# Four gate groups as a seven-product block in a hybrid decoder layer

## The chip, the cores and the metric

The kernel runs on one core of a Trainium2 chip. The metric is the device time in microseconds of one execution. TensorE (PE in the profile) multiplies matrices and accumulates into PSUM; VectorE (DVE), ScalarE (ACT) and GpSimd (POOL) work element by element; SyncE (SP) issues most of the transfers, in order, on one queue.

## The reference

One decoder layer over 1024 positions of 1024 features, in float32. Cut to what matters here:

```python
h = rms_norm(x, norm_mix_g)
y_m = mlstm_branch(h)             # 4 heads, chunks of 128 positions, state carried from chunk to chunk
y_d = diff_attention(h)           # 8 heads, causal
y_c = memory_cross_attention(h, mem)
g_m, g_d, g_c = split(sigmoid(h @ w_gate + b_gate), 3)    # w_gate is 1024 x 3072
merged = g_m*(y_m @ w_proj_m) + g_d*(y_d @ w_proj_d) + g_c*(y_c @ w_proj_c)
x = x + merged @ w_out
x = x + square(relu(rms_norm(x) @ w_up)) @ w_down
```

The gates are `h @ w_gate`, 3072 columns in 12 groups of 256 columns. Groups 0 to 3 belong to the mLSTM branch, 4 to 7 to the attention, 8 to 11 to the memory branch.

## The kernel before

Every float32 product is made of three matmuls: each operand is split into a high part (a cast on ACT to the type that TensorE multiplies fast) and a low part (a subtraction on DVE), and `mm3` adds high x high, high x low and low x high. `hT` holds the transposed h in both parts for all 8 k tiles (64 KB of each partition).

**Gate groups.** `gate_steps` is a generator: a gate group is 2 tiles of 128 columns x 2 halves of 512 positions = 4 accumulations of 8 k tiles x 3 matmuls (96 matmuls of 128x128 by 128x512), one step for each k tile. ACT takes the tanh of each accumulation and SP stores it in `gates` in HBM. The groups serve as filler for TensorE between steps of the branches that wait for other engines. `gate_steps((2, 1, 1, 2, 6))` gives the runs: groups 0 and 1 in the memory branch, 2 inside the mLSTM branch, 3 as its last part (positions 544 to 576), 4 and 5 between mLSTM branch and attention, 6 to 8 inside the attention, and 9 to 11 behind it. `gate_load` loads a group's weights and splits them (128x256 a tile).

**The mLSTM branch.** `branch_m` weaves a stream of TensorE steps with items at written-out positions (`weave`). The last of eight parts (head 0, second half) has its projections at positions 480 to 544, and its `krows`, `scores` and four `chunk`s at 528, 536 and 547 to 559. A chunk needs the split state `Ch` of the chunk ahead (tiles `C`, `Ch`) and the split weights `mpT`. The weights of all projections pass through one pool `wpm` of 25 tiles.

**The attention.** `branch_d` runs 8 heads with the projections of the next heads, then gate steps, as filler. Its pools (k and q tiles `dk`, `dq`; values `dv`; the mask; weights `daT`) lie in the memory above `hT` and the weight pools.

**The tail.** `tail` projects the three branch outputs, memory branch first. `k_tiles` loads eight y tiles of 512 KB through two buffers (`kraw`) and splits each (`kt`, ACT cast and DVE subtraction of 128x1024). The first weight group runs with its k loop outside, so that each k tile feeds 12 matmuls as it comes. Its tiles lie in the memory of `hT` and of the attention's pools. The MLP behind it already uses a form in which a 2x2 block product is made of seven products instead of eight (`PROD`, `wino`).

**Order.** Where `pinned` is set, TensorE runs in program order. Within the rest a planner orders each engine's queue, SP's and POOL's included, by program order and by its own estimate of when an instruction can start. A tile that reuses memory waits until the tiles there before it have been used for the last time; with `reuse_waits="tile"` a pool waits tile by tile.

Of the kernel before, what the change touches and what calls it, by code (L numbers as in the profile page):

```python
# [10 lines left out]
F32 = mybir.dt.float32  # L11
F32R = mybir.dt.float32r
# [19 lines left out]
def f32(ap):  # L32
    return ap.bitcast(F32)
# [38 lines left out]
class Layer:  # L72
# [359 lines left out]
    def gate_load(self, pool=None):  # L432

        pool = pool or self.gwp
        n = self.gate_n
        if n == 12 * NK:
# [131 lines left out]
    def branch_m(self, pool, gp, tail, gnext):  # L568
# [397 lines left out]
    def branch_d(self, pool):  # L966
# [143 lines left out]
                combine(s)  # L1110
        fill(8)
        norm(15, 2)
        assert self.gdone <= 288
        while self.gdone < 288:
            next(gates)
        self.pinned = False


# [497 lines left out]
    def run(self):  # L1616
        tc, nc = self.tc, self.nc
        with ExitStack() as ctx:
# [19 lines left out]
            self.x1d = dt("x1_d", (8, P, D))  # L1638
            self.h2d = dt("h2_d", (8, P, D))
            self.rd = dt("r_d", (16, P, 7, 512))  # L1640
            with ExitStack() as c1:
                E1 = lambda *x, **k: c1.enter_context(tc.tile_pool(*x, **k))
                self.pmm = E1(name="pmm", bufs=1, space=PSUM)
                self.ptp = E1(name="ptp", bufs=2, space=PSUM)
                self.psc = E1(name="psc", bufs=2, space=PSUM)
                hp = E1(name="hp", bufs=1)
                self.hT = hp.tile([P, NK, 2, S], F32R, name="hT")
                with ExitStack() as c2:
                    E2 = lambda *x, **k: c2.enter_context(tc.tile_pool(*x, **k))
                    kv = E2(name="kv", bufs=1)  # L1650
                    self.wp = E2(name="wp", bufs=4)
                    self.rp = E2(name="rp", bufs=3)
                    with tc.tile_pool(name="ptmp", bufs=1) as tmp0, tc.tile_pool(name="ptmp2", bufs=2) as tmp, tc.tile_pool(name="ptmp8", bufs=8) as tmp8:
                        class T:
                            def tile(_, shape, dt, tag, name):
                                p = tmp8 if tag == "xk" else tmp if tag in ("mx", "sq", "r1", "r4") else tmp0
                                return p.tile(shape, dt, tag=tag, name=name)
                        self.phase_x(kv, T())
                    self.gates = self.gate_steps((2, 1, 1, 2, 6))
                    with tc.tile_pool(name="pc", bufs=2) as pc, tc.tile_pool(name="pc1", bufs=1) as pc1, tc.tile_pool(name="pc3", bufs=5) as pc3, tc.tile_pool(name="pc4", bufs=6) as pc4, tc.tile_pool(name="wpc", bufs=8) as self.gwp, tc.tile_pool(name="rpc", bufs=2) as self.grp:  # L1660
                        class T2:
                            def tile(_, shape, dt, tag, name):
                                p = {"cpe": pc4, "cpT": pc3, "cscr": pc1, "gt": pc1, "cqT": pc1}.get(tag, pc)
                                return p.tile(shape, dt, tag=tag, name=name)
                        self.gpool = T2()
                        self.branch_c(T2())
                cg = ExitStack()
                gnext = cg.enter_context(tc.tile_pool(name="wgn", bufs=8, side="right"))
                with ExitStack() as c2:
                    E2 = lambda name, bufs: c2.enter_context(tc.tile_pool(name=name, bufs=bufs, reuse_waits="tile"))  # L1670
                    gm, pm3, self.rp, self.wp = E2("gm", 1), E2("pm3", 3), E2("rpm", 3), E2("wpm", 25)
                    pm1, pm = E2("pm1", 1), E2("pm", 2)
                    class T3:
                        def tile(_, shape, dt, tag, name):
                            p = pm3 if tag == "pre" else pm if tag in ("tho", "cv", "Ch", "C", "hss", "den") else pm1
                            return p.tile(shape, dt, tag=tag, name=name)
                    self.gpool, self.gwp, self.grp = T3(), self.wp, self.rp
                    self.branch_m(T3(), gm, 1, gnext)
                with tc.tile_pool(name="wpg", bufs=13, reuse_waits="tile") as self.wp, tc.tile_pool(name="rpg", bufs=3, reuse_waits="tile") as self.rp:
                    self.gwp, self.grp = self.wp, self.rp  # L1680
                    with tc.tile_pool(name="pg", bufs=2) as self.gpool:
                        for _ in range(2 * 32):
                            next(self.gates)
                    cg.close()
                    with tc.tile_pool(name="pd", bufs=2) as pd, tc.tile_pool(name="pd3", bufs=3) as pd3, tc.tile_pool(name="pdm", bufs=1) as pdm, tc.tile_pool(name="pd5", bufs=7) as pd5, tc.tile_pool(name="pdv", bufs=5) as pdv, tc.tile_pool(name="pdv2", bufs=17) as pdv2, tc.tile_pool(name="pd4", bufs=4) as pd4:
                        self.tmask = pdm.tile([P, D], F32, name="tmask")
                        nc.gpsimd.memset(self.tmask, 0.0)
                        nc.gpsimd.affine_select(
                            out=self.tmask[:, D - P : D], in_=self.tmask[:, D - P : D], pattern=[[-1, P]],
                            compare_op=ALU.is_ge, fill=NEG, base=0, channel_multiplier=1,  # L1690
                        )
                        class T4:
                            def tile(_, shape, dt, tag, name):
                                tag = "dscr2" if tag == "gt" else tag
                                p = pd5 if tag == "draw" else pdv if tag == "drr" else pdv2 if tag == "dv" else pd4 if tag in ("dk", "dkl") else pdm if tag == "dpe1" else pd3 if tag in ("daT", "dst") else pdm if tag in ("dscr", "dscr2", "y", "dsg") else pd
# [12 lines left out]
def pack(i):  # L1708
# [25 lines left out]
        return q.transpose(3, 2, 1, 0, 4)  # L1734

    wg = i["w_gate"][0]
    w["wgate"] = np.stack([grp(wg, r(256 * g, 256)) for g in range(12)])
# [33 lines left out]
```

## Time and profile before

| | |
|---|---|
| runs | 2205.79, 2208.11, 2208.55 us, median 2208.11 |
| profiled execution | 2207.4 us, of which the span from the first to the last instruction is 2205.3 |
| granted TensorE clock | 0.995 |
| busy in the span | PE 2162.5, PEld 1862.0, DVE 1360.7, ACT 982.2, POOL 525.2 us |
| HBM | read 178.76 MB, written 67.14 MB |

PEld is TensorE's weight load, which overlaps its matmuls. A row of the timeline has the start and the length in us, the engine, the line of the kernel, the operation, the tile written `<-` the tiles read with their shapes, a count where equal rows are merged, and in brackets how long the engine had been idle and what ended it. A row of a window has each engine's busy time in that stretch. A group's row ends with its count, then the busy time and the mean in ns, then the idle time ahead of it. In the view of a tile three durations are minimum, median and maximum in ns. A row of a transfer has its count, the size of one and the median us from issue to landing.

### The profile page before, as it was taken

How to read it: one execution, taken by the hardware profiler on the slowest of the kernel's cores; microseconds unless marked ns; L12 is line 12 of the kernel's file. 1: busy time of each engine (PE TensorE's matmuls, PEld its weight loads, DVE VectorE, ACT ScalarE, POOL GpSimd, SP SyncE). 2: the span in 40 equal slices, each digit the busy share in tenths (PEclk: the TensorE clock that was granted, in tenths of full speed). 3: DMA queues.
4: the chain of work that ended last, by engine and by line, in shares of the span. 5: the costliest groups of instructions: out<-in, count | busy, mean ns of one | idle time of the engine just before them, and what ended most of it. 6: DMA issues, size and time to landing. Idle time of an engine off the chain costs nothing.

```text
span 2205.3 us, 30616 instructions
## 1 busy us (share of the span) xinstructions
PE 2162.5 (98%) x11097; PEld 1862.0 (84%) x11097; DVE 1360.7 (62%) x2598; ACT 982.2 (45%) x1962; POOL 525.2 (24%) x696
## 2 busy tenths in 40 slices
PE   7999999999999999999999999999999999999999
PEld 5878888898899999999888888887787888788887
DVE  6643565565237777777641242544588877767779
ACT  6543354454336666666542120314444444543332
POOL 2100000000011111111000002102657655555553
PEclk9999999999999999999999999999999999999999
DMA  7123122121333333333343443436435444854444
GB/s 250 31 78 117 52 92 73 43 81 44 108 109 91 89 87 88 89 90 82 101 153 114 133 161 107 144 103 207 157 106 197 158 150 146 321 195 154 145 140 167
DMA packets 127948, 273.06 MB, mean 124 GB/s; under 512 B 12945, under 2 KB 21430, under 8 KB 125750
## 3 DMA queue, kind: packets, MB, share of 16 engines
q1 hardware_dynamic: 125494, 258.53, 37.2%
q10 hardware_dynamic: 2304, 12.58, 1.4%
q8 instruction: 87, 1.43, 0.3%
q14 instruction: 63, 0.52, 0.1%
HBM read 178.76 MB, written 67.14 MB: 112 GB/s over the span
## 4 chain that ended last, share of the span: by engine, by line
PE 86%; DVE 5%; DMA 4%; ACT 2%; issue 2%; POOL 1%; SPq 0%; DVEq 0%; ACTq 0%; POOLq 0%
PE mm L91 51%; PE p L91 22%; PE sc L91 6%; PE po L91 3%; PE tp L94 3%; DVE acc L67 1%; PE pr L94 1%; DVE wo L67 1%; DVE u L67 0%; DVE w L112 0%; DMA kraw<-y 0%; PE tp L91 0%; DMA wraw<-in_wdown 0%; DVE xts L67 0%; DMA xr<-h_d 0%
## 5 line engine op out<-in xcount | busy, mean ns | idle before, releaser
L91 PE MATMUL mm<-w,hT 128*128 128x384 f32 (+3 forms) x2496 | 471.7, 331 | 2.5 <-ACT w L111 2.4
L91 PE MATMUL mm<-hT,w 128*128 128x512 f32 x1920 | 465.6, 395 | 0.0
L91 PEld LDWEIGHTS mm<-hT,w 128*128 128x128 f32 x1920 | 353.6, 188 | 74.0
L91 PEld LDWEIGHTS mm<-w,hT 128*128 128x128 f32 x2496 | 389.0, 189 | 13.8 <-ACT w L111 3.2
L91 PE MATMUL p<-xo,wo 128*128 128x512 f32 x1344 | 311.0, 393 | 6.4 <-DVE st L1418 3.2
L91 PE MATMUL p<-xd,wo 128*128 128x512 f32 x1344 | 309.5, 392 | 5.5 <-DVE c L67 2.2
L91 PEld LDWEIGHTS p<-xo,wo 128*128 128x128 f32 x1344 | 253.0, 189 | 63.1 <-DVE u L67 3.7
L91 PEld LDWEIGHTS p<-xd,wo 128*128 128x128 f32 x1344 | 253.4, 189 | 61.4 <-DVE c L67 3.3
L91 PE MATMUL mm<-kt,w 128*128 128x512 f32 x1152 | 261.9, 389 | 0.9 <-DVE w L112 0.5
L112 DVE TENSOR_TENSOR w<-raw,w 128x256 fp32r<-128x256 f32 (+3 forms) x304 | 172.8, 588 | 138.2 <-ACT w L111 137.1
L91 PEld LDWEIGHTS mm<-kt,w 128*128 128x128 f32 x1152 | 216.1, 188 | 46.6 <-DVE w L112 1.0
L111 ACT CAST w<-raw 128x256 fp32r<-128x256 f32 (+3 forms) x304 | 154.4, 530 | 176.6 <-PE mm L91 132.1
L104 ACT CAST wo<-wraw 128x896 fp32r<-128x896 f32 x122 | 115.0, 944 | 213.6 <-PE p L91 101.7
L67 DVE TENSOR_TENSOR wo<-wraw,wo 128x896 fp32r<-128x896 f32 x122 | 143.3, 1192 | 58.5 <-ACT wo L104 58.5
L1145 POOL TENSOR_TENSOR wraw<-wraw 128x128 f32<-128x128 f32 x128 | 93.7, 732 | 253.1 <-DMA wraw<-in_wdown 122.9
L1007 ACT ACTIVATE dpe<-sc,dst,drr 128x256 f32<-128x256 f32 (+7 forms) x128 | 106.7, 833 | 95.5 <-DVE dst L1003 92.1
L999 DVE CUSTOM_DVE_ANT_0 sc<-sc,tmask 128x256 f32<-128x256 f32 (+7 forms) x128 | 97.0, 757 | 14.7 <-PE sc L91 14.1
L127 POOL TENSOR_SCALAR hss<-hss 128x4 f32<-128x4 f32 x8 | 3.3, 408 | 415.1 <-ACT mscr L752 273.0
L91 PE MATMUL sc<-dk,dq 128*128 128x512 f32 (+3 forms) x384 | 91.7, 347 | 0.0
L1148 POOL TENSOR_TENSOR wraw<-wraw 128x128 f32<-128x128 f32 x128 | 87.2, 681 | 9.9
L1146 POOL TENSOR_TENSOR wraw<-wraw 128x128 f32<-128x128 f32 x128 | 87.7, 685 | 0.0
L1147 POOL TENSOR_TENSOR wraw<-wraw 128x128 f32<-128x128 f32 x128 | 85.2, 665 | 0.0
(283 smaller groups left out, 2830.7 us busy)
## 6 DMA issues: line engine op xcount, KB each, us to landing
dk<-dsg SPq DMA_DIRECT2D x64, 256.0 KB, 4.2
wraw<-in_wup SPq DMA_DIRECT2D x64, 256.0 KB, 3.4
r_d<-xts SPq DMA_DIRECT2D x16, 1024.0 KB, 4.1
wraw<-in_wdown SPq DMA_DIRECT2D x64, 256.0 KB, 3.1
xd<-r_d SPq DMA_DIRECT2D x19, 768.0 KB, 7.3
xd<-r_d SPq DMA_DIRECT2D x14, 1024.0 KB, 6.7
raw<-in_wgate SPq DMA_DIRECT2D x48, 256.0 KB, 2.9
gates<-gt SPq DMA_DIRECT2D x48, 256.0 KB, 2.0
```

What stands on the lines that cost most here:

```text
L67: return self.tc.keep_in_program_order(f(*a, **k))
L91: self.pin(self.nc.tensor.matmul(out, l, r, start=start, stop=stop))
L94: self.pin(self.nc.tensor.transpose(out, x, self.ident))
L104: self.A.copy(hi, src)
L111: nc.scalar.copy(hi, src)
L112: nc.vector.tensor_sub(lo, src, f32(hi))
L999: V.tensor_tensor_reduce(out=sc[:, 0:n], in0=sc[:, 0:n], in1=self.tmask[:, D - n : D], scale=1.0, scalar=-3.0e38, op0=ALU.add, op1=ALU.max ...
L1007: nc.scalar.activation(pe[c][:, 0:n], sc[:, 0:n], AF.Exp, bias=t8[:, 2 + c : 3 + c], scale=rr[:, i, c : c + 1], accum_out=t8[:, 4 + c : 5 ...
L1145: G.tensor_add(r[:, 4], r[:, 0], r[:, 3])
L1146: G.tensor_sub(r[:, 5], r[:, 4], r[:, 1])
L1147: G.tensor_sub(r[:, 6], r[:, 1], r[:, 0])
L1148: G.tensor_sub(r[:, 7], r[:, 2], r[:, 5])
```

## The change

Groups 8 to 11 leave the generator and become a block of their own, `wino_gates`, behind the attention. The runs of the rest are (2, 1, 1, 1, 3): group 3 still ends the mLSTM branch, only group 4 stands between it and the attention, and 5 to 7 are inside the attention.

A group of the block multiplies a 2x2 block of weights with a 2x2 block of h by seven products of 4 k tiles x 3 matmuls. Products 0, 1 and 6 read h itself; the other four read sums and differences of four quarter tiles of h. These are made by `h_sums` in the mLSTM branch, in 20 portions, three positions apart from position 512 on, split into high and low parts and stored in `hcd` in HBM (8 MB); group 3's weights are now loaded at position 500. The block loads `hcd` back as four tiles of 2 MB. Sums of the weights are made on POOL, whose own queue also loads them; the seven results are combined on DVE out of two PSUM banks. The attention's and the block's pools wait tile by tile, in a new order in memory.

```diff
+        sums = self.h_sums()
+        add(500, lambda: [self.gate_load() for _ in range(NK)])
+        for i in range(20):
+            add(512 + i * 3, next, sums, None)
...
+    def h_sums(self):
+        nc, V, G = self.nc, self.nc.vector, self.nc.gpsimd
+        tl = lambda dt: self.wp.tile([P, 512], dt, tag="w", name=self.name("hs"))
+        for kp in range(4):
+            b = []
+            for q in range(4):
+                k, s = 2 * kp + q // 2, slice(q % 2 * 512, q % 2 * 512 + 512)
+                b.append(tl(F32))
+                (G if q == 3 else V).tensor_add(b[q], f32(self.hT[:, k, 0, s]), f32(self.hT[:, k, 1, s]))
+                if q % 2:
+                    yield
+            V.tensor_sub(b[1], b[0], b[1])
+            G.tensor_sub(b[0], b[2], b[0])
+            V.tensor_sub(b[2], b[2], b[1])
+            V.tensor_sub(b[3], b[3], b[2])
+            yield
+            for i, t in enumerate((b[1], b[2], b[0], b[3])):
+                hi, lo = tl(F32R), tl(F32R)
+                self.split(hi, lo, t)
+                nc.sync.dma_start(self.hcd[i, :, kp, 0:512], f32(hi))
+                nc.sync.dma_start(self.hcd[i, :, kp, 512:1024], f32(lo))
+                if i % 2:
+                    yield
+
+    def wino_gates(self, base):
...
+        gtp, ev, x3, x6, rr, x5, x4 = one("fgt", 2), one("fev", 2), one("fx3"), one("fx6"), one("fr", 3), one("fx5"), one("fx4")
+        X = {}
+        for q, p in ((4, x4), (5, x5), (6, x6), (3, x3)):
+            X[q] = p.tile([P, 4, 2, 512], F32R, tag="x", name=self.name("hx"))
+        raws, W = {}, []
+        def load(n):
+            if n < 8:
+                u, kk = divmod(n, 2)
+                r = rr.tile([P, 8, 2, P], F32, tag="fr", name=self.name("fr"))
+                for i in range(2):
+                    G.dma_start(r[:, 0:4, i], self.a["wgq"][u][:, 2 * kk + i])
+                G.tensor_add(r[:, 4], r[:, 0], r[:, 3])
+                G.tensor_sub(r[:, 5], r[:, 4], r[:, 1])
+                G.tensor_sub(r[:, 6], r[:, 1], r[:, 0])
+                G.tensor_sub(r[:, 7], r[:, 2], r[:, 5])
+                raws[n] = r
...
+        for n in range(3):
+            load(n)
+        for q in (4, 5, 6, 3):
+            nc.sync.dma_start(f32(X[q]).rearrange("p k a n -> p k (a n)"), self.hcd[q - 3])
+        for _ in range(9):
+            wsp()
+        self.pinned = True
...
+            for j, (l, q) in enumerate(self.PROD):
+                ps = self.mm_tile()
+                for kp in range(4):
+                    w = W[u * 14 + 2 * j + kp // 2]
+                    c = slice(kp % 2 * P, kp % 2 * P + P)
+                    self.mm3(ps, (w[:, 0, c], w[:, 1, c]), (x_(q, kp, 0), x_(q, kp, 1)), kp == 0, kp == 3)
+                    if kp % 2:
+                        wsp()
...
+                elif j == 5:
+                    V.tensor_add(u3, u3, ps)
+                    V.tensor_add(u2, u2, ps)
+                    out(2, u3)
+                else:
+                    V.tensor_add(u2, u2, ps)
+                    out(0, u2)
...
-                    self.gates = self.gate_steps((2, 1, 1, 2, 6))
+                    self.gates = self.gate_steps((2, 1, 1, 1, 3))
...
-                        for _ in range(2 * 32):
+                        for _ in range(32):
                             next(self.gates)
...
+                        E3 = lambda name, bufs: c3.enter_context(tc.tile_pool(name=name, bufs=bufs, reuse_waits="tile"))
+                        pdo, pdy, pdv2, pdm, pds, pd5 = E3("pdo", 2), E3("pdy", 1), E3("pdv2", 17), E3("pdm", 1), E3("pds", 1), E3("pd5", 7)
+                        pdv, pd, pd3, pd4 = E3("pdv", 5), E3("pd", 2), E3("pd3", 3), E3("pd4", 4)
...
-                    with tc.tile_pool(name="pgh", bufs=2) as self.gpool:
-                        for _ in self.gates:
-                            pass
+                    with ExitStack() as c3:
+                        self.wino_gates(c3)
```

`wsp` takes the next 256 columns of `raws` and splits them into one of 13 weight tiles, nine ahead of the products; `wgq` holds the last four groups' weights in quarters. `PROD` is `((0, 0), (1, 2), (4, 4), (5, 5), (2, 6), (3, 3), (6, 1))`: weight sum and operand of each product.

More of the change, by code (lines that the diff above doesn't have):

```diff
@@ L1112, in branch_d @@
         norm(15, 2)
-        assert self.gdone <= 288
-        while self.gdone < 288:
+        assert self.gdone <= 256
+        while self.gdone < 256:
             next(gates)
+        self.pinned = False
+    def h_sums(self):
[21 more added lines that the diff above has]
+                    yield
@@ new lines, in wino_gates, with wsp, x_, out @@
+    def wino_gates(self, base):
+        nc, V, A, G = self.nc, self.nc.vector, self.nc.scalar, self.nc.gpsimd
+        one = lambda name, bufs=1: base.enter_context(tc.tile_pool(name=name, bufs=bufs, reuse_waits="tile"))
+        tc = self.tc
+        gtp, ev, x3, x6, rr, x5, x4 = one("fgt", 2), one("fev", 2), one("fx3"), one("fx6"), one("fr", 3), one("fx5"), one("fx4")
[14 more added lines that the diff above has]
+                raws[n] = r
+        def wsp():
+            n = len(W)
+            if n < 56:
+                u, r = divmod(n, 14)
+                j, kk = divmod(r, 2)
+                t = self.wp.tile([P, 2, 256], F32R, tag="w", name=self.name("w"))
+                self.split(t[:, 0], t[:, 1], raws[2 * u + kk][:, 1 + self.PROD[j][0]].rearrange("p k n -> p (k n)"))
+                W.append(t)
+                if j == 6:
+                    load(2 * u + 3 + kk)
+        def x_(q, kp, i):
+            if q >= 3:
+                return X[q][:, kp, i]
+            k, hf = divmod(q + 1, 2)
+            return self.hT[:, 2 * kp + k, i, hf * 512 : hf * 512 + 512]
+        for n in range(3):
[5 more added lines that the diff above has]
+        self.pinned = True
+        tl = lambda n: ev.tile([P, 512], F32, tag=n, name=self.name(n))
+        for u in range(4):
+            def out(i, c):
+                ft, s = 16 + u * 2 + i // 2, slice(i % 2 * 512, i % 2 * 512 + 512)
+                t = gtp.tile([P, 512], F32, tag="gt", name=self.name("gt"))
+                A.activation(t, c, AF.Tanh, bias=self.bg[:, ft : ft + 1], scale=0.5)
+                nc.sync.dma_start(self.gdr[ft, :, s], t)
+            for j, (l, q) in enumerate(self.PROD):
[6 more added lines that the diff above has]
+                        wsp()
+                if j == 0:
+                    u2, c11, u3, c21 = (tl(n) for n in ("u2", "c11", "u3", "c21"))
+                    A.copy(u2, ps)
+                elif j == 1:
+                    V.tensor_add(c11, u2, ps)
+                    out(1, c11)
+                elif j == 2:
+                    V.tensor_add(u2, u2, ps)
+                elif j == 3:
+                    V.tensor_add(u3, u2, ps)
+                elif j == 4:
+                    V.tensor_add(c21, u3, ps)
+                    out(3, c21)
+                elif j == 5:
[3 more added lines that the diff above has]
+                else:
+                    V.tensor_add(u2, u2, ps)
+                    out(0, u2)
@@ L1736, in pack @@
     wg = i["w_gate"][0]
-    w["wgate"] = np.stack([grp(wg, r(256 * g, 256)) for g in range(12)])
+    w["wgate"] = np.stack([grp(wg, r(256 * g, 256)) for g in range(8)])
+    w["wgq"] = quads(wg[:, 2048:])
     for n, s in (("wpm", "w_proj_m"), ("wpd", "w_proj_d"), ("wpc", "w_proj_c"), ("wout", "w_out")):
```

10 lines of the change are left out of this document (7 added, 3 removed).

## The prediction

> **What bounds the kernel now.** I read the page first (busy shares, slices, chain), then the timeline around the two places that the change touches, the windows there, and the tile and transfer views for durations.
>
> ```profile
> span 2205.3 us, 30616 instructions
> PE 2162.5 (98%) x11097; PEld 1862.0 (84%) x11097; DVE 1360.7 (62%) x2598; ACT 982.2 (45%) x1962; POOL 525.2 (24%) x696
> ...
> GB/s 250 31 78 117 52 92 73 43 81 44 108 109 91 89 87 88 89 90 82 101 153 114 133 161 107 144 103 207 157 106 197 158 150 146 321 195 154 145 140 167
> ...
> PE 86%; DVE 5%; DMA 4%; ACT 2%; issue 2%; POOL 1%; SPq 0%; DVEq 0%; ACTq 0%; POOLq 0%
> ```
>
> TensorE is busy for 98% of the span and carries 86% of the chain that ended last; 42.8 us of the span are without a matmul. So a matmul that disappears is worth its whole pitch, as long as the operands still come in time. The pitch stands in the timeline of the last gate group (four accumulations of 24 matmuls, each ended by one tanh), and in the windows of the three stages:
>
> ```profile
> 1189.20 0.69 ACT L471 ACTIVATE gt<-mm,dv 128x512 f32<-128x512 f32 x1 [3.04 <-PE mm L91]
> ...
> 1210.96 0.69 ACT L471 ACTIVATE gt<-mm,dv 128x512 f32<-128x512 f32 x1 [4.75 <-PE mm L91]
> core 0: us, PE busy (x) PEld busy (x) DVE busy (x) ACT busy (x) POOL busy (x), PEclk, DMA share, GB/s
> 1144.00:1211.00 67.00, 67.00 (x298) 55.45 (x297) 11.41 (x20) 18.33 (x33) 0.06 (x1) 1.00 0.36 123
> 533.00:576.00 43.00, 43.00 (x227) 36.40 (x226) 12.11 (x35) 14.54 (x38) 1.20 (x2) 1.00 0.14 49
> ```
>
> 21.76 us for 96 matmuls is 0.2267 us each, at a granted clock of 1.00. Behind the attention (1144 to 1211) PE never pauses, and DVE works 11.4 of 67 us. In the last 43 us of the mLSTM branch PE never pauses either, and DVE works 12.1.
>
> **The change part by part.**
>
> *The products (gain).* Four groups of 4 x 24 matmuls become four of 7 x 12: 336 for 384. 48 x 0.2267 = 10.9 us less on the engine that sets the end. The block lasts 336 x 0.2267 = 76.2 us, a product 2.72 us.
>
> *The block's own side work.* Prices:
>
> ```profile
> L112 DVE TENSOR_TENSOR w<-raw,w 128x256 fp32r<-128x256 f32 x184 | 72.5, 419 | 50.6 <-ACT w L111 50.5
> L112 DVE TENSOR_TENSOR w<-raw,w 128x384 fp32r<-128x384 f32 x64 | 34.5, 553 | 32.4 <-ACT w L111 31.5
> L67 DVE TENSOR_TENSOR c<-u,p 128x512 f32<-128x512 f32 x30 | 20.6, 685 | 21.6 <-ACT u L1199 19.6 <-PE p L91 0.6
> L1145 POOL TENSOR_TENSOR wraw<-wraw x128: 450/463/2507, 1407.3 to 2181.7; 128x128 f32<-128x128 f32 x128
> L1128 POOL TENSOR_TENSOR xts<-rq x16: 1288/1798/2132, 1620.8 to 1912.3; 128x512 f32<-128x512 f32 x16
> L67 DVE TENSOR_TENSOR xts<-rq,xts x32: 693/837/1676, 1621.5 to 1911.1; 128x512 f32<-128x512 f32 x32
> ```
>
> 56 weight splits x 0.42 = 23.5 us and 28 combining adds x 0.69 = 19.2 us put 42.7 us on DVE in 76.2: it fits. POOL adds 32 sums of 128x256, each between the 0.46 of 128 elements and the 1.29 of 512: 15 to 41 us. What can reach PE is the emptying of PSUM: two banks, so product j+2 waits until DVE has emptied j, within 2.72 us; the sixth needs two adds (1.4 us), and a weight split or a POOL sum can stand ahead of them. Ends: 0 (1.4 below 2.7), and 1 us on each of four sixth products, 4 us. I take 0.5, nearer the lower end, since DVE is idle 44% of the time. POOL also issues 16 transfers, an operation the trace does not hold; by SP's issue of 0.3 us and POOL's longest tensor operation of 2.1 us that is 5 to 34 us of POOL, beside the sums still under 76.2. [...]
>
> *The operand sums in the mLSTM branch.* Per two k tiles: DVE 3 adds, 3 subtractions, 4 low halves; ACT 4 casts; POOL 2; SP 8 stores of 256 KB. Four times over: DVE 40 x 0.69 = 27.6 us, POOL 8 x 1.29 = 10.3, 32 stores on SP's queue. They need slots of the 25-tile weight pool, which head 0's values give back from about 533 on; before that DVE cannot start them in earnest. ACT, 14.5 of 43 us busy, has room. DVE has 12.1 + 27.6 = 39.7 us to do in 43, where PE's next chunk waits for it:
>
> ```profile
> 544.45 0.69 DVE L112 TENSOR_TENSOR mpT<-ngb,mpT 128x512 fp32r<-128x512 f32 x1 [0.69 <-ACT mpT L111]
> ...
> 550.95 0.52 PE L91 MATMUL sc<-va,mpT 128*128 128x258 f32 x3
> ...
> 551.87 0.48 DVE L740 SCALAR_TENSOR_TENSOR C<-C,g_dec,sc 128x258 f32<-128x258 f32 x1 [6.74 <-PE sc L91]
> ...
> 552.83 0.43 DVE L112 TENSOR_TENSOR Ch<-C,Ch 128x258 fp32r<-128x258 f32 x1 [0.48 <-ACT Ch L111]
> ...
> 555.20 0.52 PE L91 MATMUL sc<-Ch,qp 128*128 128x258 f32 x3
> ```
>
> mpT is ready 5.8 us ahead of its use, but the state Ch only 1.94 us (553.26 to 555.20). One foreign 0.69 us operation ahead of C and one ahead of the low half (1.4 us) still fit; a third does not. The portions are spaced by three steps (about 2.1 us), and a portion holds at most three DVE operations, so a backlog from the slots, handed to DVE ahead of C since it is earlier in the program, is what costs. Ends: 0, and a backlog of seven operations less the slack, about 3 us, met twice: 6 us. I take 2. PE's queue is in program order, so what waits behind is everything. The stores: 2.0 us each to landing (row below), 8.4 MB in 40 us beside 49 GB/s: hidden; SP's y and gate stores queue behind them, with a group of 21.8 us still to come before the attention.
>
> *One group less ahead of the attention.* The cover for the attention's first weights shrinks from 43.5 us (two groups) to 21.8. They need three loads and eight splits of 128x384, 8 x 0.55 = 4.4 us of DVE after a transfer (384 KB, so less than the 4.2 us of 512 KB below): taken at nothing. If DVE comes 12 us late out of the sums, the cover is gone and PE waits for the excess.
>
> *The operands' way back.* Four loads of 2 MB on SP's queue, into memory of the attention's k, q, mask and v tiles.
>
> ```profile
> 1110.05 1.10 PE L91 MATMUL sc<-dk,dq 128*128 128x512 f32 x4
> ...
> 1124.96 1.03 PE L91 MATMUL po<-dv,daT 128*128 128x128 f32 x7 [0.33 <-DVE daT L112]
> 1143.58 0.60 PE L94 MATMUL tp<-ident,doS 128*128 128x128 f32 x4
> kraw<-y SPq DMA_DIRECT2D x24, 512.0 KB, 4.2
> xr<-h_d SPq DMA_DIRECT2D x4, 1024.0 KB, 5.3
> r_d<-xts SPq DMA_DIRECT2D x16, 1024.0 KB, 4.1
> xd<-r_d SPq DMA_DIRECT2D x14, 1024.0 KB, 6.7
> gates<-gt SPq DMA_DIRECT2D x48, 256.0 KB, 2.0
> ```
>
> The last reads of k and q end at 1111, those of v at 1126, the block starts at 1144. 2 MB is 8.2 us by r_d's row, 10.6 by xr's, 13.4 by xd's. One behind the other from 1111 they end at 1153.5 by xr's; the first is needed at 1149.4, the fourth at 1157.6: hidden. By xd's row the fourth is 7 us late. I take 0, as the slice at 321 GB/s (6.5 us for 2 MB) shows that the queue moves more than these single rows. If a load sits at SP's head waiting for a tile, the gate stores behind it wait, and by the two gate buffers the tanh and PE.
>
> *The tail's entry.* Before, five of the eight y tiles of the memory branch were loaded and split under the last groups:
>
> ```profile
> 1155.49 0.33 SPq L1268 DMA_DIRECT2D kraw<-y  x1
> 1159.17 1.05 ACT L111 CAST kt<-kraw 128x1024 fp32r<-128x1024 f32 x1 [3.44 <-DMA kraw<-y]
> 1160.25 1.23 DVE L112 TENSOR_TENSOR kt<-kraw,kt 128x1024 fp32r<-128x1024 f32 x1 [3.66 <-ACT kt L111]
> 1161.51 2.48 SPq L1268 DMA_DIRECT2D kraw<-y  x2
> ```
>
> Now that memory holds the block's operands. Adding up the tiles from the code, the first y buffer begins 0.5 KB before the end of operand 6's, and the first y tile lies in it; operand 6 is last read by the fifth of seven products, 2 x 2.72 = 5.4 us before the block's end. From there: 3.7 to the cast, 1.05, 1.23 (1155.49 to 1161.48, 6.0): the first tile is ready 0.6 us, with the hand-overs about 1 us, after the block. Two buffers then give two tiles every 6.0 us, while PE eats two in 24 x 0.2267 = 5.4: three more waits of 0.6. Together 2.8; ends 1 (the low half not needed by the first matmul) and 6 (landings of 4.2 and more beside weights and gates). I take 3.
>
> *Sum* against the profiled execution (2207.4 us: span 2205.3 and 2.1 around it; the median of the runs, 2208.1, lies 0.7 above): -10.9 + 0.5 + 2 + 0 + 3 = -5.4, so 2202.0 profiled and 2202.7 as a median.
>
> **The rivals.**
> 1. *All hidden.* The planner fits sums and loads into idle time, or runs the sums behind the mLSTM branch, under the remaining group, so that they are not where the change says. For: 31 of 43 us of DVE are free. Against: the first y tile. -10.9 + 1 = 2198.2.
> 2. *DVE and POOL in each other's way.* The xts rows show a DVE subtraction of 0.69 us lasting 1.68 beside a POOL one, and the POOL one 2.13 for 1.29. If each of eight POOL sums holds DVE for its 1.29 us, the branch needs 12.1 + 27.6 + 10.3 = 50 us in 43; with the 7 us over on PE, 3.5 at the other places: -0.4, 2207.7. Against: the overrun can slide under the next group. [...]
> 3. *The tail waits for the whole block.* If the first y load goes out only when all of the block's memory is given back, the first tile is 6.1 us late and 1.8 follow: -10.9 + 7.9 + 2.5 = 2207.6. It decides whether that load is issued ahead of the last product.
> 4. *Slower: the operands are fetched only once the attention has ended.* If the four loads stand on SP's queue behind the attention's last stores, the fourth lands 4 x 8.2 = 32.8 us after 1144, and is needed after 13.6: PE waits 19.2; with 5.5 elsewhere 2221.9. Against: the memory is free from 1111 and 1126 on. It turns into a loss against before once the fourth lands later than 19 us after the attention.
>
> **How the numbers follow.** My forecast 50%, its own range 2199 to 2205; rival 1 13%, rival 2 15%, rival 3 9%, rival 4 13%. 0.2%, some 4.4 us, is about what a measurement can tell here; so faster means up to 2203.7. Faster: rival 1 and 42 of the forecast's 50 points, 55%. Slower: rival 4, and 3 points of rival 2 with more waits than priced, 16%. The same: the rest, 29%. The range 2197 to 2213 takes in all but rival 4 and those points.
>
> **What would show it.** Products: 48 matmuls fewer, the block 76 us. Mid-branch: PE gaps between 533 and 576 released by DVE C, Ch or mpT, 2 us in all; 7 or more is rival 2. Loads: the operand transfers issued from about 1111; after 1144 is rival 4. Tail: the first matmul on a y tile about 1 us after the block's last, then gaps of 0.6 released by the y tiles' low halves; 6 us is rival 3. The forecast fails if the gaps at these three places add up to less than 2 or more than 9 us, or if a gap opens inside the attention.

## The result, and the profile after

The changed kernel is slower: 2233.6 us median (2228.5 to 2234.6, 4 runs) against 2207.4 (4 runs) for the kernel before on the same chip, ratio 1.0114 (95% interval 1.0097 to 1.0132). The profiled execution took 2234.1 us. Page of the changed kernel (span and busy times, transfer queues, chain):

```profile
span 2232.3 us, 30835 instructions
PE 2164.0 (97%) x11049; PEld 1859.6 (83%) x11049; DVE 1422.9 (64%) x2690; ACT 1002.3 (45%) x2006; POOL 579.5 (26%) x752
...
q0 software_dynamic: 1280, 4.20, 0.6%
...
PE 79%; DVE 8%; DMA 5%; issue 3%; ACT 2%; POOL 2%; SPq 0%; DVEq 0%; ACTq 0%; POOLq 0%
```

The row q0 is POOL's queue, which the kernel before doesn't use. TensorE issues 48 matmuls less (11049 for 11097), as the change says. Yet it is not busy for less time (2164.0 for 2162.5), its share of the chain fell from 86 to 79%, and 68 us of the span are without a matmul instead of 43. So matmuls became slower in places, and gaps came. The timeline of PE shows where (a gap stands in brackets, with what ended it):

```profile
553.54 0.51 PE L91 MATMUL sc<-va,mpT 128*128 128x258 f32 x2 [1.50 <-ACT mpT L111]
555.04 0.39 PE L91 MATMUL sc<-va,mpT 128*128 128x258 f32 x1 [0.98 <-DVE mpT L112]
562.49 1.01 PE L91 MATMUL sc<-Ch,qp 128*128 128x258 f32 x3 [1.64 <-ACT Ch L111]
567.80 0.51 PE L91 MATMUL sc<-Ch,qp 128*128 128x258 f32 x2 [0.68 <-DVE Ch L112]
...
607.19 18.91 PE L91 MATMUL mm<-w,hT 128*128 128x384 f32 x108
...
1098.77 1.10 PE L91 MATMUL sc<-dk,dq 128*128 128x512 f32 x4
...
1141.14 6.76 PE L91 MATMUL mm<-hT,w 128*128 128x512 f32 x18 [12.78 <-ACT gt L471]
1147.74 0.60 PE L94 MATMUL tp<-ident,doS 128*128 128x128 f32 x4
...
1160.13 9.98 PE L91 MATMUL mm<-hx,w 128*128 128x512 f32 x36 [2.21 <-DVE c L1214]
1183.61 10.06 PE L91 MATMUL mm<-hx,w 128*128 128x512 f32 x36 [2.62 <-DVE c L1214]
1207.08 10.08 PE L91 MATMUL mm<-hx,w 128*128 128x512 f32 x36 [2.54 <-DVE c L1214]
```

Four places: gaps in the mLSTM branch; one of 12.8 us while the last gate group runs at the attention's end; one of about 2.5 us in each of the block's first three groups; and, behind the four longest of these gaps, matmuls that take longer (18 in 6.76 us, where 18 undisturbed ones take 4.31, from 1104.57 on; 36 in 9.98 to 10.08, where 36 take 8.32 from 1169.94 on).

To compare runs, the start of the same matmul is taken in each profile: the first `sc<-va,mpT` behind 300 us, the first 128x384 matmul (the attention's first), the last `sc<-dk,dq`, the last `tp<-ident,doS`, and the first matmul on a `kt`. What lies between two of them is a stage. Where a gate group less lies in the stage, the value before is shortened by 21.76 us. Example, the attention's end: 1147.74 - 1098.77 = 48.97 us after; before 1143.58 - 1110.05 = 33.53; 15.4 more. For the block and the tail's entry the value before is 67.13 us and the seven-product block adds 76.16 - 65.28 = 10.88, so 78.0 is what it would be without any wait. Us above before, or above those 78.0:

| run | median us | mLSTM branch and group 4 | attention | attention's end | block and tail's entry |
|---|---|---|---|---|---|
| after | 2233.6 | 7.9 | 1.4 | 15.4 | 14.7 |
| 1: loads on SP | 2207.7 | 8.0 | 1.6 | 0.0 | 3.1 |
| 2: no sums | 2230.6 | -0.4 | 1.2 | 13.7 | 13.1 |
| 3: loads on SP, no sums | 2202.9 | -0.1 | 1.6 | 0.0 | 3.2 |
| 4: loads on SP, sums in group 4 | 2217.2 | 10.8 | 6.3 | 0.0 | 3.4 |
| 5: POOL loads, long pieces | 2207.8 | 7.9 | 1.3 | 4.5 | 1.7 |
| 6: POOL loads, setting of 4096 | 2213.3 | 7.8 | 3.2 | 2.0 | 0.0 |
| 7: loads on SP, sums halved | 2203.8 | -0.1 | 3.9 | 0.0 | 3.3 |
| 8: as 7, operand 4 moved | 2200.9 | -0.2 | 4.0 | 0.0 | 2.1 |
| 9: POOL loads, tanh first | 2232.1 | 7.6 | 1.2 | 0.5 | 28.8 |
| 10: loads on SP, sums all on DVE | 2197.3 | 0.4 | 1.3 | 0.0 | 3.5 |
| 11: POOL loads, sums all on DVE | 2224.3 | 0.4 | 1.2 | 15.5 | 14.1 |
| 12: as 10, operand 4 moved | 2199.4 | 0.3 | 1.3 | 0.0 | 1.4 |

Outside these stages the first 312 us differ between the profiles by -2.3 to +6.6 us; one profile each can't tell why. The tail behind the first `kt` differs from before by -5.8 (run 9) to +3.4 us (run 6), and is 2.7 us shorter after. Much of that arises at one place that no run edits, the MLP's first long wait and the matmuls behind it (PE before, then after):

```profile
1580.59 17.34 PE L91 MATMUL p<-xo,wo 128*128 128x512 f32 x63 [3.15 <-DVE st L1418]
1610.27 14.55 PE L91 MATMUL p<-xo,wo 128*128 128x512 f32 x63 [1.80 <-DVE st L1532]
```

Wait and row together are 4.1 us shorter after. Why the wait differs stays open.

**The late weights.** Timeline of POOL's queue after, then the transfers that it issues, and the casts on ACT that wait for them:

```profile
1112.57 0.95 POOL L1163 DMA_DIRECT2D fr<-in_wgq  x1 [29.62 <-PE tp L94]
1121.04 0.78 POOL L1163 DMA_DIRECT2D fr<-in_wgq  x1 [7.52 <-issue]
...
1129.51 0.79 POOL L1163 DMA_DIRECT2D fr<-in_wgq  x1 [7.42 <-issue]
...
1133.10 0.81 POOL L1163 DMA_DIRECT2D fr<-in_wgq  x1 [1.74 <-issue]
1136.66 0.75 POOL L1163 DMA_DIRECT2D fr<-in_wgq  x1 [2.76 <-issue]
1137.43 0.91 POOL L1164 TENSOR_TENSOR fr<-fr 128x256 f32<-128x256 f32 x1
```

```profile
hx<-hc_d SPq DMA_DIRECT2D x4, 2048.0 KB, 10.4
fr<-in_wgq POOLq DMA_DIRECT2D x16, 256.0 KB, 3.3
```

```profile
1129.28 0.40 ACT L111 CAST w<-fr 128x256 fp32r<-128x256 f32 x1 [11.06 <-DMA fr<-in_wgq]
1136.43 1.02 ACT L111 CAST w<-fr 128x256 fp32r<-128x256 f32 x3 [6.75 <-DMA fr<-in_wgq]
1140.10 0.40 ACT L111 CAST w<-fr 128x256 fp32r<-128x256 f32 x1 [2.65 <-POOL fr L1165]
1140.41 0.68 ACT L471 ACTIVATE gt<-mm,dv 128x512 f32<-128x512 f32 x1
```

The issues stand 8.5, 8.5, 3.6 and 3.6 us apart, while one keeps POOL busy for only 0.8. The casts date the landings: the first weight tile needs the first two transfers and is cast at 1129.28, and POOL's third issue follows at 1129.51; the second tile's second transfer ends at 1136.43, and the fifth issue follows at 1136.66. By the landings in the trace, 12 of the 15 later issues begin 0.3 us after the transfer before them has landed, and the other three 7.8 us or more after it: POOL never has two in flight here. In the first 17 us a landing takes 8.2 us (the longest in the source view), beside the 2 MB operand loads; afterwards 3.3. POOL's sums of the first tile stand in its queue behind the fifth issue, so they start only at 1137.43. The gate tanh (1140.41) is queued on ACT behind the casts, so PSUM isn't emptied and PE stands.

The block's gaps come the same way. For the first of them, ACT and then DVE:

```profile
1158.61 0.71 ACT L111 CAST w<-fr 128x256 fp32r<-128x256 f32 x2 [5.20 <-DMA fr<-in_wgq]
1159.05 0.43 DVE L112 TENSOR_TENSOR w<-fr,w 128x256 fp32r<-128x256 f32 x1 [5.67 <-ACT w L111]
1159.39 0.68 DVE L1214 TENSOR_TENSOR c<-u,mm 128x512 f32<-128x512 f32 x1
```

The add that empties PSUM (L1214) stands on DVE behind the split of a later weight tile, and that split waits for the transfer issued at 1155.23; PE goes on at 1160.13, when the add is done.

**The mLSTM branch.** Windows (columns PE, PEld, DVE, ACT, POOL busy, granted clock, share of the transfer engines, GB/s) and the timeline of DVE after:

```profile
545.00:563.00 18.00, 13.77 (x58) 10.71 (x56) 15.62 (x27) 6.58 (x14) 6.26 (x5) 0.91 0.46 173
```

```profile
544.49 1.52 DVE L1131 TENSOR_TENSOR hs<-hT 128x512 f32<-128x512 f32 x1
...
548.67 1.77 DVE L1136 TENSOR_TENSOR hs<-hs,hs 128x512 f32<-128x512 f32 x1 [1.20 <-POOL hs L1135]
...
552.17 0.67 DVE L711 TENSOR_TENSOR ngb<-ngb,tp 128x512 f32<-128x512 f32 x1
...
554.30 0.68 DVE L112 TENSOR_TENSOR mpT<-ngb,mpT 128x512 fp32r<-128x512 f32 x1
...
559.24 1.76 DVE L1136 TENSOR_TENSOR hs<-hs,hs 128x512 f32<-128x512 f32 x1 [1.18 <-POOL hs L1135]
...
561.52 0.47 DVE L740 SCALAR_TENSOR_TENSOR C<-C,g_dec,sc 128x258 f32<-128x258 f32 x1
```

`mpT` ends at 554.98 instead of 545.14, and the first `C` of this part comes at 561.52 instead of 551.87. Ahead of both, DVE waits 0.8 to 1.2 us for each POOL subtraction and takes 1.5 to 1.8 us for single operations that alone take 0.68. Over the whole branch, four such waits come to 4.0 us, and four such long operations to 3.9 us more than undisturbed.

### The profile page after: what moved, and what is told of

The parts are those of the page before. It is cut to its first block, busy times and chain, and to the rows that moved or that the text cites. A ratio compares the mean times of both kernels' runs of the same rounds, so it can differ in the third digit from the quotient of the medians.

```text
span 2232.3 us, 30835 instructions
## 1 busy us (share of the span) xinstructions
PE 2164.0 (97%) x11049; PEld 1859.6 (83%) x11049; DVE 1422.9 (64%) x2690; ACT 1002.3 (45%) x2006; POOL 579.5 (26%) x752
## 4 chain that ended last, share of the span: by engine, by line
PE 79%; DVE 8%; DMA 5%; issue 3%; ACT 2%; POOL 2%; SPq 0%; DVEq 0%; ACTq 0%; POOLq 0%
PE mm L91 45%; PE p L91 22%; PE sc L91 6%; PE po L91 3%; PE tp L94 3%; DMA kraw<-y 1%; DVE acc L67 1%; DVE w L112 1%; DVE wo L67 1%; PE pr L94 1%; DMA x_d<-gl 1%; DVE u L67 0%; DMA fr<-in_wgq 0%; DMA gl<-in_xT 0%; DVE hs L1131 0%
## 5 line engine op out<-in xcount | busy, mean ns | idle before, releaser
L91 PE MATMUL mm<-hT,w 128*128 128x512 f32 x1680 | 416.0, 399 | 12.8 <-ACT gt L471 12.8
L91 PEld LDWEIGHTS mm<-hT,w 128*128 128x128 f32 x1680 | 311.3, 190 | 78.7 <-ACT gt L471 13.2
L111 ACT CAST w<-raw 128x256 fp32r<-128x256 f32 (+3 forms) x272 | 142.3, 544 | 151.4 <-PE mm L91 124.5
L112 DVE TENSOR_TENSOR w<-raw,w 128x256 fp32r<-128x256 f32 (+3 forms) x272 | 159.9, 609 | 77.6 <-ACT w L111 74.1
L1259 POOL TENSOR_TENSOR wraw<-wraw 128x128 f32<-128x128 f32 x128 | 96.2, 751 | 246.7 <-DMA wraw<-in_wdown 88.6
L1003 DVE CUSTOM_DVE_ANT_0 sc<-sc,tmask 128x256 f32<-128x256 f32 (+7 forms) x128 | 97.1, 759 | 14.7 <-PE sc L91 14.0
L1262 POOL TENSOR_TENSOR wraw<-wraw 128x128 f32<-128x128 f32 x128 | 87.8, 686 | 10.0
L1261 POOL TENSOR_TENSOR wraw<-wraw 128x128 f32<-128x128 f32 x128 | 88.1, 688 | 0.0
```

The costliest lines, as they stand in the source:

```text
L91: self.pin(self.nc.tensor.matmul(out, l, r, start=start, stop=stop))
L111: nc.scalar.copy(hi, src)
L112: nc.vector.tensor_sub(lo, src, f32(hi))
L1003: V.tensor_tensor_reduce(out=sc[:, 0:n], in0=sc[:, 0:n], in1=self.tmask[:, D - n : D], scale=1.0, scalar=-3.0e38, op0=ALU.add, op1=ALU.max ...
L1259: G.tensor_add(r[:, 4], r[:, 0], r[:, 3])
L1261: G.tensor_sub(r[:, 6], r[:, 1], r[:, 0])
```

## The experiments

**Whose queue issues the weight loads (run 1).**

```diff
-                    G.dma_start(r[:, 0:4, i], self.a["wgq"][u][:, 2 * kk + i])
+                    nc.sync.dma_start(r[:, 0:4, i], self.a["wgq"][u][:, 2 * kk + i])
```

> Only the queue of the block's 16 weight loads changes: SyncE issues them instead of GpSimd. Theory A (the GpSimd issues hold GpSimd for 3.6 to 8.5 us each, the weights come late, and casts of them stand ahead of the gate tanh on ScalarE and ahead of the adds on VectorE): the 12.8 us gap at the attention's end and the three gaps of 2.2 to 2.6 us in the block go, and with them about 5 us of lowered TensorE clock: 2207 to 2213 us, and the block lasts 76 to 79 us instead of 89. Rival: the weights are late because their memory comes free late or because the four operand loads take the transfer engines; then the gap at the attention's end stays at 8 us or more, 2228 us or above. Rival for the clock: it falls in any run of this block; then the time is 2213 to 2218.

Measured: 2207.7 us, ratio to before 1.0006 (0.9994 to 1.0019). The gap at the attention's end and those of the block are gone, and so are the slow matmuls there. SP issues the first four loads at once, 7 us later than POOL began, behind three of the operand loads and ahead of the fourth, and a landing takes 3.0 to 5.0 us:

```profile
1119.88 3.01 SPq L1163 DMA_DIRECT2D fr<-in_wgq  x4
```

Some 26 us, the whole loss, hang on the queue of 16 transfers. It does not say yet what about that queue, as the order beside the operand loads has changed too.

**The sums' operations left out (runs 2 and 3).** `h_sums` keeps its 32 stores, but stores pieces of `hT` in place of the sums; in run 3 the loads are on SP as well.

```diff
-                (G if q == 3 else V).tensor_add(b[q], f32(self.hT[:, k, 0, s]), f32(self.hT[:, k, 1, s]))
...
-                nc.sync.dma_start(self.hcd[i, :, kp, 0:512], f32(hi))
-                nc.sync.dma_start(self.hcd[i, :, kp, 512:1024], f32(lo))
+                nc.sync.dma_start(self.hcd[i, :, kp, 0:512], f32(self.hT[:, k, 0, s]))
+                nc.sync.dma_start(self.hcd[i, :, kp, 512:1024], f32(self.hT[:, k, 1, s]))
```

> Leaves out the adds, subtractions and splits of the operand sums (the 32 stores stay and write plain pieces of the normalised input instead); the loads stay on GpSimd. Theory B (the sums' operations on VectorE and ScalarE stand ahead of mpT, C and Ch of the mLSTM branch): the group after the branch starts at 576 to 578 us instead of 584.7, and the time falls by 7 to 9 us, 2225 to 2227 us. Rival: the delay comes from the stores or from the other order of the weight loads; then the group starts at 583 or later and the time stays within 3 us of 2233.6.

> Both edits: loads on SyncE, and the sums' operations left out (stores of plain pieces of the input stay). If A and B are all that is wrong and they add up: 2199 to 2204 us, that is the sum of the prediction without the sums. Rival: a third cost (the tail's entry, the block's own PSUM emptying) is larger than 4 us; then 2206 us or more.

Measured: 2230.6 and 2202.9 us. In both profiles the branch's 8 us are gone (the table's first stage: -0.4 and -0.1), so the operations cost them and not the stores. The group behind the branch starts at 581.9 us in run 2, where 576 to 578 was expected, and the times fell by only 3.0 and 4.8, less than the 7 to 9 expected of run 2: both profiles lose 4.5 to 6.6 us in the first 312 us, ahead of anything that was edited, over 2 of it between 40 and 80 us, which accounts for the later group. Where that loss comes from isn't explained.

**The sums after the branch (run 4).** The 20 portions run beside the steps of gate group 4, with tiles of the weight pool there; loads on SP.

> Loads on SyncE; the sums stay whole, but are made in 20 portions in the gate group after the mLSTM branch (21.8 us, VectorE 9 of 44 us busy there) instead of in the branch. Theory: the branch loses its 8 us delay, the group's own PSUM is emptied by four tanh only, so the sums cost nothing there: 2200 to 2205 us. Rival: the 28 us of sums on VectorE run past the 21.8 us of the group and stand ahead of the splits of the attention's first weights; then TensorE waits 5 to 12 us at the attention's first matmul, 2207 to 2214 us.

Measured: 2217.2 us, the rival, and 3 us above its range. The attention's first matmul:

```profile
607.45 0.69 PE L91 MATMUL mm<-w,hT 128*128 128x384 f32 x1 [10.97 <-ACT w L111]
```

ACT's casts of the attention's weights stand behind those of the sums, which end at 606.98. The cover of one gate group that the prediction took as enough for 4.4 us of splits isn't enough for 28 us of sums.

**Long pieces, and a larger setting (runs 5 and 6): what about POOL's queue.** Both leave the loads on POOL. In run 5 the tile's layout makes a transfer of 256 KB of 128 pieces of 2 KB, where it was 512 pieces of 512 B; in run 6 the pieces stay, the program's `dynamic_dma_scratch_size` grows from 1024 to 4096, and a pool of weight tiles has 12 instead of 13.

```diff
-                r = rr.tile([P, 8, 2, P], F32, tag="fr", name=self.name("fr"))
+                r = rr.tile([P, 2, 8, P], F32, tag="fr", name=self.name("fr"))
...
-                    G.dma_start(r[:, 0:4, i], self.a["wgq"][u][:, 2 * kk + i])
+                    G.dma_start(r[:, i, 0:4], self.a["wgq"][u][:, 2 * kk + i])
```

```diff
-    nc = bacc.Bacc("TRN2", target_bir_lowering=False, num_devices=1, dynamic_dma_scratch_size=1024)
+    nc = bacc.Bacc("TRN2", target_bir_lowering=False, num_devices=1, dynamic_dma_scratch_size=4096)
```

> The loads stay on GpSimd; only the layout of the weight tile changes, so that each transfer of 256 KB is 128 pieces of 2 KB instead of 512 of 512 B. Theory P (in the trace after, the second issue begins 0.3 us after the first transfer has landed, and the third after the second: GpSimd can't issue until the earlier transfer's pieces have left its queue): with a quarter of the pieces the first six issues go out within 10 us instead of 28, the 12.8 us gap at the attention's end shrinks to 0 to 3 us, the time falls to 2207 to 2215 us. Rival Q (an issue on GpSimd takes its 3.6 to 8.5 us by itself, or by its bytes): the spacing and the time stay, 2228 us or more.

> [...] Theory P: the same as with long pieces: the issues stand at most 1.5 us apart where nothing else holds GpSimd, 2207 to 2215 us. Rival Q: spacing and time stay, 2228 us or more. [...]

Measured: 2207.8 us (ratio to before 1.0000, 0.9991 to 1.0009) and 2213.3 us. Timelines of POOL and PE in run 5:

```profile
1111.03 1.31 POOL L1163 DMA_DIRECT2D fr<-in_wgq  x2 [29.66 <-PE tp L94]
...
1115.86 0.58 POOL L1163 DMA_DIRECT2D fr<-in_wgq  x1 [0.28 <-issue]
...
1117.47 1.16 POOL L1163 DMA_DIRECT2D fr<-in_wgq  x2
```

```profile
1129.40 5.97 PE L91 MATMUL mm<-hT,w 128*128 128x512 f32 x18 [2.59 <-ACT gt L471]
```

and in run 6:

```profile
1111.87 1.72 POOL L1163 DMA_DIRECT2D fr<-in_wgq  x2 [29.27 <-PE tp L94]
```

```profile
1129.31 4.40 PE L91 MATMUL mm<-hT,w 128*128 128x512 f32 x18 [1.68 <-ACT gt L471]
```

Now the second issue follows the first without a pause. POOL's "issue" idle time ahead of these transfers falls from 40.7 us in all to 0.4 and 0.6. The operand loads go out as in the changed kernel, the last at 1117.11 and 1117.93, so their traffic doesn't explain it. Two independent edits bear theory P out: with a quarter of the pieces the first two issues take 1.31 us together and a landing 3.0 at the least, with four times the setting 1.72 and 3.2, so two transfers are in flight. That the queue lacked room for pieces, and not speed, is the author's reading of this; how many it has room for was not shown. ACT's order is instruction for instruction the same in run 5 as in the changed kernel, and the 12.8 us gap shrinks to 2.6. Run 6 is 5.5 us slower than run 5 all the same (2.8 in the profiled executions). It has one weight tile less (12 for 13), and its attention takes 1.9 us longer; but its first `kt` matmul comes 3.4 us earlier (1211.57 against 1214.95), and the tail behind that takes 5.9 us more. Of these, 4.4 arise at the MLP's wait named above: 3.90 us for 1.80, and 16.90 for 14.56 in the 63 matmuls behind it. What lengthens that wait was not tested.

**ACT's order (run 9).** The tanhs of the last gate group are kept ahead of the first nine casts; the planner then put all of that group, and the last `yd`, first.

> The loads stay on GpSimd with 512-byte pieces, as late as in the changed kernel; only ScalarE's queue differs: the last gate group's tanhs are kept in front of the casts of the block's first weights. If the queue order is what turns the late weights into the 12.8 us gap: that gap goes, and TensorE waits instead at the block's first two or three products, since the second weight tile lands at about 1136 us and GpSimd's sums of it follow until 1143: 4 to 9 us there, the three gaps of 2.2 to 2.6 us inside the block stay, 2224 to 2230 us. If the weights alone set the time, wherever the wait stands: 2231 us or more.

Measured: 2232.1 us, not told apart from the 2233.6 of the changed kernel, so the late weights set the time, wherever the wait stands. The 12.8 us gap is gone and came back behind it. Timeline of PE (lines are one further on in this kernel):

```profile
1135.37 1.67 PE L92 MATMUL mm<-hT,w 128*128 128x512 f32 x6 [1.12 <-ACT w L67]
1137.82 0.73 PE L92 MATMUL mm<-hT,w 128*128 128x512 f32 x2 [0.79 <-ACT w L67]
...
1147.28 10.63 PE L92 MATMUL mm<-hx,w 128*128 128x512 f32 x36 [4.60 <-ACT u L1218]
...
1166.08 4.38 PE L92 MATMUL mm<-hx,w 128*128 128x512 f32 x12 [8.17 <-DVE u L1225]
```

The two last stages together are 29.3 us, against 30.1 in the changed kernel.

**Half of the sums (run 7), and operand 4 in operand 6's memory (run 8).** Loads on SP. Ten portions stay in the branch, six positions apart; ten go beside group 4, in a pool of their own.

```diff
-        for i in range(20):
-            add(512 + i * 3, next, sums, None)
+        for i in range(10):
+            add(512 + i * 6, next, sums, None)
```

```diff
-        gtp, ev, x3, x6, rr, x5, x4 = one("fgt", 2), one("fev", 2), one("fx3"), one("fx6"), one("fr", 3), one("fx5"), one("fx4")
+        gtp, ev, x3, x4, rr, x5, x6 = one("fgt", 2), one("fev", 2), one("fx3"), one("fx4"), one("fr", 3), one("fx5"), one("fx6")
```

> Loads on SyncE; the first half of the sums stays in the mLSTM branch with twice the spacing, the second half goes into the gate group behind it, with memory of its own. Theory B (what costs is the backlog on VectorE ahead of mpT, C and Ch; 14 us of sums fit in, 28 don't): the delay in the branch falls from 8 us to 1 to 4, no wait over 1 us at the attention's first matmuls: 2200 to 2205 us. Rival: any sums ahead of C cost their full length; then the branch loses 5 us or more and the time is 2206 us or more.

> As the run with the sums halved, and operand 4 (last read by the third of the seven products) takes the memory of operand 6 (last read by the fifth), so that the first y tile of the tail can come 5.4 us earlier. If the tail's first wait is that memory: the 1.7 us ahead of the first matmul on a y tile goes to 0 to 0.5, and 1 to 3 us less in all than without: 2198 to 2204 us. Rival: the y tile waits for something else (the queue, its own landing); then no difference, within 1 us.

Measured: 2203.8 (ratio 0.9981, 0.9972 to 0.9990) and 2200.9 us (0.9973, 0.9963 to 0.9984). Half of the sums cost the branch nothing; the other half costs the attention 2.6 us (3.9 against 1.3), with gaps of 0.96 and 1.08 at its start. With the operand moved, PE goes from the block to the first `kt` without a gap (1.3 us in run 7), and that stage is 1.2 us shorter. The two medians, 2.9 us apart, aren't told apart by their runs (2197.7 to 2206.0 and 2195.4 to 2206.5).

**All sums on DVE (runs 10 and 11).** The 8 operations that POOL did go to DVE, which gets 5.5 us more to do; run 10 has the loads on SP, run 11 on POOL.

```diff
-                (G if q == 3 else V).tensor_add(b[q], f32(self.hT[:, k, 0, s]), f32(self.hT[:, k, 1, s]))
+                V.tensor_add(b[q], f32(self.hT[:, k, 0, s]), f32(self.hT[:, k, 1, s]))
...
-            G.tensor_sub(b[0], b[2], b[0])
+            V.tensor_sub(b[0], b[2], b[0])
```

> Loads on SyncE, all sums in the mLSTM branch as in the changed kernel, but the 8 of their operations that GpSimd does are done by VectorE (8 x 0.69 = 5.5 us more work on VectorE). If VectorE and GpSimd hold each other up (rival 2 of the prediction), the branch's delay of 8.1 us does not grow, 4 to 8 us, and the time stays at 2203 to 2208 us. If only VectorE's amount of work counts, the delay grows to 11 to 14 us: 2210 to 2214 us.

> The changed kernel with one edit: the 8 sum operations of GpSimd are done by VectorE; the weight loads stay on GpSimd with 512-byte pieces. With the loads on SyncE this edit brought 10.4 us (2207.7 to 2197.3). If the two causes are independent: 2222 to 2226 us, no gap in the mLSTM branch, and the 12.8 us gap and the three gaps in the block unchanged. If the late weights absorb what the branch gains: 2229 us or more.

Measured: 2197.3 us (ratio to before 0.9949, 0.9934 to 0.9964), below both values expected, and 2224.3. The window and DVE's timeline of run 10:

```profile
545.00:563.00 18.00, 17.89 (x93) 14.97 (x92) 18.00 (x41) 9.83 (x26) 0.00 (x0) 1.00 0.67 249
```

```profile
545.79 0.68 DVE L112 TENSOR_TENSOR mpT<-ngb,mpT 128x512 fp32r<-128x512 f32 x1
...
549.47 2.49 DVE L1131 TENSOR_TENSOR hs<-hT 128x512 f32<-128x512 f32 x4
551.88 0.48 DVE L740 SCALAR_TENSOR_TENSOR C<-C,g_dec,sc 128x258 f32<-128x258 f32 x1
```

DVE has more to do and is done earlier: 18.00 of 18 us busy without a wait, `C` at 551.88, PE without a gap. So not the amount of VectorE's work cost the 8 us, but POOL's part in it. The waits (4.0 us) and the long operations (3.9) of the changed kernel are gone. The planner also ordered DVE's queue differently: of the second pair of k tiles all 10 DVE operations stand ahead of `mpT` in the changed kernel, and 8 of 12 in run 10. How much of the 8 us is the wait, the slowing or the order is not shown. The two causes add up: 9.3 us for the sums and 25.9 for the loads alone make 35.2, and 36.3 were measured together.

**All three repairs (run 12).**

> All three repairs: loads on SyncE, all sums on VectorE, operand 4 in the memory of operand 6. The swap took 2.9 us off where the sums were halved (2203.8 to 2200.9). If it adds up: 2194 to 2197 us, and the first matmul on a y tile follows the block's last within 0.5 us instead of 1.6. Rival: the swap's gain was chance, or lay in the earlier stages; then 2197 to 2199 us.

Measured: 2199.4 us (ratio 0.9962, 0.9950 to 0.9975), 0.4 us above the rival's range and above what adding up would give. The first `kt` matmul does follow at once and its stage is 2.1 us shorter than in run 10, but that profile also starts 2.9 us later at 312 us. Run 12 isn't told apart from run 10; both are faster than the kernel before and than the change.

## Why the prediction was wrong

- *The products, -10.9.* Right: 48 matmuls less, and with the loads on SP the stage of the block fits 76.2 us and 3.1 of waits.
- *"POOL also issues 16 transfers ... 5 to 34 us of POOL, beside the sums still under 76.2."* This step failed, and with it the forecast: taken at nothing, it cost 25.9 us. The bound took an issue for work of POOL, by SP's issue and POOL's longest tensor operation; 0.8 us busy was inside it. (POOL's longest operation in the rows shown there is 2.5 us, of `wraw`, and not 2.1; that would only have raised the upper end to 40.) What it left out is that the next issue can wait for the landing of the last, 8.2 us beside the operand loads. And 76.2 us was the wrong room: the block's first group needs two weight tiles, and their four transfers have to land between the attention's last use of that memory (1112.57) and the end of its last gate group, which without the 15.4 us lost would have been at about 1133. One behind the other they take 2 x 8.5 + 3.6 + 3.3 = 24 us, more than the 20 there are, and the sums and casts come only behind that. Three loads ahead, as in the code, is no cover for this: three ahead is the very stretch that came late.
- *The sums in the branch, +2 (0 to 6).* Too low: 7.9. The 0 came from counting DVE's work at its undisturbed 0.69 us, where 39.7 of 43 us fit. That count was sound (run 10 gets in 5.5 us more without delay), so the backlog from the slots, which the step named, isn't the cause. Rival 2 had it: 7 us over in the branch, by DVE and POOL in each other's way, with the rows of 0.69 us that lasted 1.68. It got 15% and was kept out of the sum. The hs rows (1.52 and 1.77 us for 0.68) and run 10 (0.4 us lost in the branch) agree with it; by what means one engine slows the other was not shown.
- *The operands' way back, 0.* Right: issued from 1100 on (1111 was forecast), landed before their use, and no wait for them shows. Rival 4, the only slower case, did not happen. But the loads kept the transfer engines full just when the weights were due (a share of 0.97 and 372 GB/s from 1100 to 1126 us after).
- *One group less ahead of the attention, 0.* Right for the change (607.19 without a gap); run 4 shows what it costs once sums come in front.
- *The block's own side work, 0.5, and the tail's entry, 3.* About right together: 3.1 to 3.5 us in runs 1, 3, 4, 7 and 10, where 3.5 was forecast, but split otherwise: in runs 1, 7 and 10 PE waits 1.0 to 1.5 us for PSUM at the block's third product, and 1.3 to 1.7 ahead of the first `kt`. The reason given, memory of operand 6, is borne out by 1.2 and 2.1 us less once it is moved.
- *Not in the sum:* the attention takes 1.2 to 1.6 us more in most runs, with one gap of 0.5 to 0.8 us in which PE waits for DVE's `dsg`; not tried further.

With the two failed terms put right (25.9 more and 5.9 more) the sum would have been 2202.0 + 31.8 = 2233.8 profiled; 2234.1 was measured. That checks the list more than the method, since both terms are measured here, and it is that close partly by chance: the attention's 1.4 and the shorter tail stand against each other.

## What to carry to other kernels

A transfer moved to another queue is priced by when its data land in the stretch that needs them first, not by the engine's busy time over the whole stage; ask how many such transfers that queue can have in flight, and count the pieces of each (here one of 512 pieces, and at least two of 128). Where the trace shows no transfer of that queue, take one landing for each issue as the upper end of the estimate; here that was 8.2 us beside the operand loads and 3.3 behind them. And work split over VectorE and GpSimd in one chain can take longer than all of it on VectorE (here 7.9 us lost in the branch, and 0.4): add the waits on each other and the stretched rows, before counting idle time as room.

## What the hardware showed that was not expected

Behind a gap the granted clock can fall for some us. At the end of the 12.8 us gap and behind it, the windows of 4 us from 1134 to 1146 show 0.50, the next one 0.97, and 18 matmuls take 6.76 us for 4.31. Behind the gap of 2.59 us in run 5 the next window shows 0.59, and 18 take 5.97:

```profile
1130.00:1134.00 4.00, 4.00 (x12) 3.14 (x11) 2.57 (x5) 1.80 (x4) 3.89 (x5) 0.59 0.22 81
```

Behind the 1.68 us of run 6 the same window stays at 1.00 (18 in 4.40). Gaps close together can count too: behind 1.50 and 0.98 us with two matmuls between them, in the changed kernel's window of 0.91 above, 12 matmuls take 4.51 us, and 2.94 at 563.33. But length alone doesn't decide. In run 9 two gaps of 2.70 and 2.72 us cost 0.16 us more each: 24 matmuls take 5.76 us behind the first, for 5.60 undisturbed (run 4, from 1159.82 on), and 36 behind the second take 8.48 for 8.32:

```profile
1207.38 8.48 PE L92 MATMUL mm<-hx,w 128*128 128x512 f32 x36 [2.72 <-DVE c L1220]
```

In the changed kernel the row behind 2.54 us takes 10.08, and the window from 1208 to 1212 shows 0.61. So a gap of 2 to 3 us can cost about 1.6 us again, or next to nothing, and no run here shows what decides it; the prediction priced gaps at their length alone.
